# A batched matrix product on one core: paired transposes, a manual order and a rearranged end

## The chip, the cores and the metric

The kernel runs on one core of a Trainium2 chip. The metric is the device time of one execution in microseconds, the median of the runs. Before the change it is 530.44 us (12 runs, 529.81 to 531.82).

## What is computed

The reference multiplies 32 pairs of matrices, all in float32 in memory:

```python
batch, m, k, n = 32, 512, 1024, 768
def reference(x, weight):        # x: 32 x 512 x 1024, weight: 32 x 1024 x 768
    return np.matmul(x, weight).astype(np.float32)
```

A batch reads 2.10 MB of x and 3.15 MB of weights and writes 1.57 MB. Over 32 batches that is 167.77 MB read and 50.33 MB written.

## The kernel before

The batches are worked off in one loop (L51). For each batch, GpSimd issues two transfers that cast to bfloat16 on the way: the weights into `wb_sb` (L53) and x into `x_sb` (L56). Each has three buffers, so loads run up to three batches ahead; a load into a used buffer waits until TensorE has read that buffer for the last time. The weights are laid out with 8 consecutive rows of k on each of the 128 partitions, and x with 4 consecutive rows of m, so a partition reads one contiguous piece of memory per transfer.

A batch consists of four row tiles of 128 rows (the loop over `mt`, L60). TensorE needs x with k on the partitions. So it transposes eight 128x128 blocks of the row tile against an identity matrix (L64), each into its own PSUM tile `pt`, and each is copied to `xT_sb` at once (L69). Then eight matmuls add up 512 output columns in the PSUM tile `pm`, and eight more the other 256 (L74), and each sum is copied to `out_sb` (L81). The copies are given to `nc.any`: the scheduler puts them on VectorE or ScalarE, which decides the order of the instructions on each engine as well. After the four row tiles, SP issues one store of the whole batch (L83). The output tile has three buffers.

[...]

Of the kernel before, what the change touches and what calls it, by code (L numbers as in the profile page):

```python
# [1 line left out]

# [5 lines left out]

F32 = mybir.dt.float32
BF16 = mybir.dt.bfloat16  # L10


@with_exitstack
def kernel(
    ctx: ExitStack,
    tc: tile.TileContext,
    x: bass.AP,
    weight: bass.AP,
    out: bass.AP,
):  # L20
    nc = tc.nc
    B, M, K = x.shape
    _, _, N = weight.shape
    P = 128
    assert M % P == 0 and K % P == 0
    MT = M // P
    KT = K // P

    N_SPLITS = []
    off = 0  # L30
    while off < N:
        sz = min(512, N - off)
        N_SPLITS.append((off, sz))
        off += sz

    const = ctx.enter_context(tc.tile_pool(name="const", bufs=1))
    ident = const.tile([P, P], BF16)
    make_identity(nc, ident)

    w_pool = ctx.enter_context(tc.tile_pool(name="w", bufs=3))  # L40
    x_pool = ctx.enter_context(tc.tile_pool(name="x", bufs=3))
    xT_pool = ctx.enter_context(tc.tile_pool(name="xT", bufs=4))
    out_pool = ctx.enter_context(tc.tile_pool(name="out", bufs=3))
    tpsum = ctx.enter_context(tc.tile_pool(name="tpsum", bufs=4, space=bass.MemoryType.PSUM))
    mpsum = ctx.enter_context(tc.tile_pool(name="mpsum", bufs=4, space=bass.MemoryType.PSUM))

    w_view = weight.rearrange("b (ki ko) n -> b ki ko n", ki=P)
    x_view = x.rearrange("b (mi mo) k -> b mi mo k", mi=P)
    out_view = out.rearrange("b (mi mo) n -> b mi mo n", mi=P)

    for b in range(B):  # L51
        wb_sb = w_pool.tile([P, KT, N], BF16)
        nc.gpsimd.dma_start(out=wb_sb, in_=w_view[b])  # L53

        x_sb = x_pool.tile([P, MT, K], BF16)
        nc.gpsimd.dma_start(out=x_sb, in_=x_view[b])  # L56

        out_sb = out_pool.tile([P, MT, N], F32)

        for mt in range(MT):  # L60
            xT_sb = xT_pool.tile([P, KT, P], BF16)
            for j in range(KT):
                pt = tpsum.tile([P, P], BF16)
                nc.tensor.transpose(  # L64
                    pt,
                    x_sb[:, mt, j::KT],
                    ident,
                )
                nc.any.tensor_copy(xT_sb[:, j, :], pt)  # L69

            for (noff, nsz) in N_SPLITS:
                pm = mpsum.tile([P, nsz], F32)
                for j in range(KT):
                    nc.tensor.matmul(  # L74
                        pm,
                        xT_sb[:, j, :],
                        wb_sb[:, j, noff:noff + nsz],
                        start=(j == 0),
                        stop=(j == KT - 1),
                    )  # L80
                nc.any.tensor_copy(out_sb[:, mt, noff:noff + nsz], pm)  # L81

        nc.sync.dma_start(out_view[b], out_sb)  # L83


# [1 line left out]
_INS = ['x', 'weight']  # L87
_OUTS = [((32, 512, 768), 'float32')]


# [23 lines left out]
```

## Time and profile before

| what | value |
|---|---|
| median of 12 runs | 530.44 us |
| profiled execution, its time | 530.53 us |
| profiled execution, its span | 528.7 us |
| TensorE matmuls busy | 434.7 us, 82% |
| TensorE weight loads busy | 287.8 us, 54% |
| VectorE / ScalarE busy | 103.2 us, 20% / 222.6 us, 42% |
| mean granted TensorE clock | 0.970 |
| bytes written by the DMA engines | 134.72 MB, mean 255 GB/s |
| weights transfer, issue to landing | 34.0 us median |
| store, issue to landing | 14.5 us median |

The span is the time from the first to the last instruction of the profiled execution; its device time is 1.85 us longer. Busy times of matmuls are modelled, so 82% does not say that TensorE runs at 82% of its peak. The GB/s of the page count what lands: a load of float32 that is cast to bfloat16 counts half of what it reads. A DMA share is the mean busy share of the 16 DMA engines; as records of neighbouring packets overlap a little, it can stand slightly above 1.

### The profile page before, as it was taken

To read this page: it belongs to the slowest core of one execution; us is meant where nothing else is said; L and a number is where in the kernel's file an instruction comes from. 1 tells how busy PE (TensorE), PEld (TensorE's weight loads), DVE (VectorE), ACT (ScalarE), POOL (GpSimd) and SP (SyncE) were. 2 spreads that over 40 slices of the span, in tenths; PEclk is the share of its full clock that TensorE was granted. 3 is DMA by queue.
4 is the path that set the end of the run, shared out by engine and by line. 5 is a ranking of instruction groups with operands and counts; after the bars stand their busy time and mean duration, and the time that the engine had idled before them with its cause. 6 is when DMAs were issued, how large, how long until landed. Compare 5 with 4: busy or idle time off the path is not lost.

```text
span 528.7 us, 7878 instructions
## 1 busy us (share of the span) xinstructions
PE 434.7 (82%) x3015; PEld 287.8 (54%) x3072; DVE 103.2 (20%) x515; ACT 222.6 (42%) x766; POOL 34.6 (7%) x70
## 2 busy tenths in 40 slices
PE   0799979877799879789897979788889977988794
PEld 0466656555466556456465656556555654655463
DVE  0122211212122111122121121212121121221111
ACT  0254534444354434345353444434443443444342
POOL 3000000000000000000000000000000000000000
PEclk9999999999899989999898999989998998999899
DMA  8999999999999999999999999999999999999952
GB/s 160 216 222 277 276 262 269 274 274 262 250 254 275 273 270 244 268 257 276 273 249 270 245 274 274 273 261 249 262 267 277 258 269 255 255 273 275 267 189 120
DMA packets 13861, 134.72 MB, mean 255 GB/s; under 512 B 1536, under 2 KB 1536, under 8 KB 1536
## 3 DMA queue, kind: packets, MB, share of 16 engines
q0 software_dynamic: 9216, 83.89, 75.6%
q1 hardware_dynamic: 4608, 50.33, 23.0%
q8 instruction: 24, 0.39, 0.3%
q14 instruction: 13, 0.11, 0.0%
HBM read 167.77 MB, written 50.33 MB: 413 GB/s over the span
## 4 chain that ended last, share of the span: by engine, by line
issue 81%; DMA 9%; POOL 6%; PE 2%; POOLq 0%; DVE 0%; ACT 0%
DMA wb_sb<-in_weight_dram 7%; POOL wb_sb L53 3%; POOL x_sb L56 3%; DMA x_sb<-in_x_dram 3%; PE pm L74 2%; PE pt L64 0%; DVE xT_sb L69 0%; POOLq L53 0%; POOLq L56 0%; ACT out_sb L81 0%; POOL ident masks.py:199 0%; POOL ident masks.py:197 0%; POOLq masks.py:199 0%; POOLq L109 0%; POOLq L98 0%
## 5 line engine op out<-in xcount | busy, mean ns | idle before, releaser
L74 PE MATMUL pm<-wb_sb,xT_sb 128*128 128x512 bf16 (+1 forms) x1991 | 382.2, 334 | 47.5 <-DMA wb_sb<-in_weight_dram 44.4
L74 PEld LDWEIGHTS <-xT_sb 128*128 128x128 bf16 x2048 | 200.4, 100 | 158.1 <-issue 48.9
L81 ACT COPY out_sb<-pm 128x512 f32<-128x512 f32 (+1 forms) x256 | 122.5, 479 | 207.4 <-PE pm L74 192.9
L69 DVE COPY xT_sb<-pt 128x128 bf16<-128x128 bf16 x515 | 103.2, 221 | 417.0 <-PE pt L64 402.7
L64 PE MATMUL pt<-ident,x_sb 128*128 128x128 bf16 x1024 | 126.4, 226 | 40.0 <-DVE xT_sb L69 22.3
L69 ACT COPY xT_sb<-pt 128x128 bf16<-128x128 bf16 x509 | 112.0, 273 | 92.0 <-PE pt L64 91.6
L64 PEld LDWEIGHTS <-x_sb 128*128 128x128 bf16 x1024 | 102.1, 148 | 76.2 <-issue 48.8
L56 POOL DMA_DIRECT2D x_sb<-in_x_dram x32 | 17.0, 530 | 385.5 <-PE pt L64 385.5
L53 POOL DMA_DIRECT2D wb_sb<-in_weight_dram x32 | 17.1, 533 | 54.2 <-PE pt L64 53.8
L69 ACT ACT_TABLE_LOAD x1 | 1.3, 1283 | 0.7 <-PEq L98 0.7
masks.py:199 POOL TENSOR_SCALAR_AFFINE_SELECT ident<-ident 128x128 bf16<-128x128 bf16 x1 | 0.3, 305 | 0.1
masks.py:197 POOL MEMSET ident<- 128x128 bf16 x1 | 0.2, 204 | 0.3 <-POOLq L98 0.3
L98 POOL MEMSET const-float32-0.0<- 128x1 f32 x1 | 0.1, 98 | 0.2 <-issue 0.2
L98 POOL MEMSET const-bfloat16-1.0<- 128x1 bf16 x1 | 0.1, 101 | 0.0
L98 POOL MEMSET const-uint8-127<- 128x1 uint8 x1 | 0.1, 101 | 0.0
L98 POOL MEMSET const-float32-1.0<- 128x1 f32 x1 | 0.1, 98 | 0.0
## 6 DMA issues: line engine op xcount, KB each, us to landing
wb_sb<-in_weight_dram POOLq DMA_DIRECT2D x32, 1536.0 KB, 34.0
out_dram<-out_sb SPq DMA_DIRECT2D x32, 1536.0 KB, 14.5
x_sb<-in_x_dram POOLq DMA_DIRECT2D x32, 1024.0 KB, 27.3
```

The lines of the kernel that those rows point to most:

```text
L53: nc.gpsimd.dma_start(out=wb_sb, in_=w_view[b])
L56: nc.gpsimd.dma_start(out=x_sb, in_=x_view[b])
L64: nc.tensor.transpose(pt, x_sb[:, mt, j::KT], ident,)
L69: nc.any.tensor_copy(xT_sb[:, j, :], pt)
L74: nc.tensor.matmul(pm, xT_sb[:, j, :], wb_sb[:, j, noff:noff + nsz], start=(j == 0), stop=(j == KT - 1),)
L81: nc.any.tensor_copy(out_sb[:, mt, noff:noff + nsz], pm)
L98: nc = _bacc.Bacc("TRN2", target_bir_lowering=False, num_devices=1)
```

## The change

The kernel fixes the order by hand (`manual_schedule`) and changes these things:

- **Transposes.** x in bfloat16 is read as pairs, one 4-byte float32 element for two neighbours in k. Four transposes of 128x128 four-byte elements into one PSUM bank take the place of eight two-byte ones (L64 of the new kernel). One copy on VectorE of 1024 two-byte elements takes the whole row tile out of PSUM (L66). The two members of a pair lie next to each other there, so a matmul reads its weights with a step of two elements.
- **PSUM and eviction.** Two row tiles share three PSUM banks (1536 columns). ScalarE copies out the first 1024 columns, VectorE the last 512, once for each pair of row tiles. The 512-column and 256-column matmuls alternate.
- **Buffers and order of loads.** x, weights and output have five buffers instead of three. x comes before the weights of its batch, and the loads of batch b + 4 are issued at the start of batch b. The identity is made after batch 0's loads are issued.
- **The last four batches.** Their weights are loaded in chunks of rows, two of four rows each, for the last batch four, two and two. All four row tiles work through a chunk before the next chunk begins, into two PSUM tiles at once. The transposes of the next batch stand between the row tiles of the last chunk. The stores of batches 28, 29 and 30 are issued by GpSimd behind the last load. The last batch is stored by SP in two halves, one for each pair of row tiles.

The core of the diff:

```diff
+    CHUNKED = {B - 4: (4, 4), B - 3: (4, 4), B - 2: (4, 4), B - 1: (4, 2, 2)}
+    HELD = {B - 4, B - 3, B - 2}
...
+    def load_w(b):
+        ws[b] = w_pool.tile([P, KT, N], BF16, name="w_sb")
+        at = 0
+        for n in CHUNKED.get(b, (KT,)):
+            nc.gpsimd.dma_start(out=ws[b][:, at:at + n, :], in_=w_view[b, :, at:at + n, :])
+            at += n
...
+    def transpose(b, mt):
+
+        pt = tpsum.tile([P, JT, P], F32, name="pt")
+        pairs = xs[b].bitcast(F32)
+        for j in range(JT):
+            nc.tensor.transpose(pt[:, j, :], pairs[:, mt, j::JT], ident)
+        xT = xT_pool.tile([P, JT, P, 2], BF16, name="xT")
+        nc.vector.tensor_copy(
+            xT.rearrange("p j m r -> p (j m r)"), pt.bitcast(BF16).rearrange("p j m -> p (j m)")
+        )
+        return xT
...
+    def evacuate(b, pair, pm):
+        o = outs[b]
+        nc.scalar.copy(o[:, pair * N2:pair * N2 + 1024], pm[:, 0:1024])
+        nc.vector.tensor_copy(o[:, pair * N2 + 1024:(pair + 1) * N2], pm[:, 1024:N2])
...
+        for b in range(B):
+            if b + 4 < B:
+                load_x(b + 4)
+                load_w(b + 4)
+            outs[b] = out_pool.tile([P, MT * N], F32, name="out_sb")
+            if b not in CHUNKED:
+                xT = {mt: transpose(b, mt) for mt in (0, 1)}
+                for pair in range(2):
+                    pm = mpsum.tile([P, N2], F32, name="pm")
+                    for half in range(2):
+                        if pair == 0:
+                            matmuls(pm, half, xT[half], b, range(KT), False)
+                            xT[2 + half] = transpose(b, 2 + half)
+                        else:
+                            matmuls(pm, half, xT[2 + half], b, range(KT), False)
+                    evacuate(b, pair, pm)
+                nc.sync.dma_start(out_view[b], outs[b])
+                continue
+            xT = ready.pop(b, None) or {mt: transpose(b, mt) for mt in range(MT)}
+            pms = [mpsum.tile([P, N2], F32, name="pm") for _ in range(2)]
+            at = 0
+            for n in CHUNKED[b]:
+                last = at + n == KT
+                for mt in range(MT):
+                    if last and b + 1 < B:
+                        ready.setdefault(b + 1, {})[mt] = transpose(b + 1, mt)
+                    matmuls(pms[mt // 2], mt % 2, xT[mt], b, range(at, at + n), True)
+                    if last and mt % 2 == 1:
+                        pair = mt // 2
+                        evacuate(b, pair, pms[pair])
+                        if b not in HELD:
+                            cols = slice(pair * N2, (pair + 1) * N2)
+                            nc.sync.dma_start(out_view[b, :, cols], outs[b][:, cols])
+                at += n
+            if b in HELD:
+                nc.gpsimd.dma_start(out=out_view[b], in_=outs[b])
```

More of the change, by code (lines that the diff above doesn't have):

```diff
@@ L24 @@
     P = 128
-    assert M % P == 0 and K % P == 0
     MT = M // P
     KT = K // P
[L29 to L34, printed above, removed]
-    const = ctx.enter_context(tc.tile_pool(name="const", bufs=1))
[L37 to L42, printed above, removed]
@@ L43 @@
-    out_pool = ctx.enter_context(tc.tile_pool(name="out", bufs=3))
-    tpsum = ctx.enter_context(tc.tile_pool(name="tpsum", bufs=4, space=bass.MemoryType.PSUM))
-    mpsum = ctx.enter_context(tc.tile_pool(name="mpsum", bufs=4, space=bass.MemoryType.PSUM))
+    JT = KT // 2
+    N2 = 2 * N
+    CHUNKED = {B - 4: (4, 4), B - 3: (4, 4), B - 2: (4, 4), B - 1: (4, 2, 2)}
+    HELD = {B - 4, B - 3, B - 2}
+    const = ctx.enter_context(tc.tile_pool(name="const", bufs=1))
+    w_pool = ctx.enter_context(tc.tile_pool(name="w", bufs=5))
@@ L47 @@
+    x_pool = ctx.enter_context(tc.tile_pool(name="x", bufs=5))
+    xT_pool = ctx.enter_context(tc.tile_pool(name="xT", bufs=8))
+    out_pool = ctx.enter_context(tc.tile_pool(name="out", bufs=5))
+    tpsum = ctx.enter_context(tc.tile_pool(name="tpsum", bufs=2, space=bass.MemoryType.PSUM))
+    mpsum = ctx.enter_context(tc.tile_pool(name="mpsum", bufs=2, space=bass.MemoryType.PSUM))
     w_view = weight.rearrange("b (ki ko) n -> b ki ko n", ki=P)
     x_view = x.rearrange("b (mi mo) k -> b mi mo k", mi=P)
-    out_view = out.rearrange("b (mi mo) n -> b mi mo n", mi=P)
@@ L51 @@
[L51 to L67, printed above, removed]
-                )
[L69 to L83, printed above, removed]
+    out_view = out.rearrange("b (mi mo) n -> b mi (mo n)", mi=P)
@@ new lines, with load_x @@
+    xs, ws, outs = {}, {}, {}
+    def load_x(b):
+        xs[b] = x_pool.tile([P, MT, K], BF16, name="x_sb")
+        nc.gpsimd.dma_start(out=xs[b], in_=x_view[b])
+    def load_w(b):
[14 more added lines that the diff above has]
+        return xT
@@ new lines, with matmuls @@
+    SPLITS = (((0, 512), (512, N - 512)), ((0, 1024 - N), (1024 - N, N2 - 1024)))
+    def matmuls(pm, half, xT, b, kos, together):
+        for ko in kos:
+            for i, (off, size) in enumerate(SPLITS[half]):
+                shares = half == 1 and i == 0
+                nc.tensor.matmul(
+                    pm[:, half * N + off:half * N + off + size],
+                    xT[:, ko // 2, :, ko % 2],
+                    ws[b][:, ko, off:off + size],
+                    start=(ko == 0 and not (together and shares)),
+                    stop=(ko == KT - 1),
+                    skip_group_check=together,
+                )
@@ new lines, in evacuate @@
+    def evacuate(b, pair, pm):
+        o = outs[b]
+        nc.scalar.copy(o[:, pair * N2:pair * N2 + 1024], pm[:, 0:1024])
+        nc.vector.tensor_copy(o[:, pair * N2 + 1024:(pair + 1) * N2], pm[:, 1024:N2])
+    with tc.manual_schedule():
+        load_x(0)
+        load_w(0)
+        ident = const.tile([P, P], F32)
+        make_identity(nc, ident)
+        for b in range(1, 4):
+            load_x(b)
+            load_w(b)
+        ready = {}
+        for b in range(B):
[34 more added lines that the diff above has]
+                nc.gpsimd.dma_start(out=out_view[b], in_=outs[b])
```

## The prediction

> **What bounds the kernel now.** I read the page's slices first: which resource is full, and where it stops being full. Then the queue table, the windows cut at the places where the DMA row changes, the waits, and last TensorE's rows inside one batch. From the page, slices and queue table:
>
> ```profile
> PE   0799979877799879789897979788889977988794
> DMA  8999999999999999999999999999999999999952
> ...
> q0 software_dynamic: 9216, 83.89, 75.6%
> q1 hardware_dynamic: 4608, 50.33, 23.0%
> HBM read 167.77 MB, written 50.33 MB: 413 GB/s over the span
> ```
>
> The DMA row is full from the second slice to the third last and then drops to 5 and 2. TensorE has 7s and 8s throughout. The two queues add up to 98.6% of 16 engines' span, that is 521.3 us of packet time per engine in a span of 528.7. No edit that leaves the bytes alone can take much from the middle. The windows (columns: length, busy time and count of PE, PEld, DVE, ACT, POOL, then clock, DMA share, GB/s) show what is left at the end:
>
> ```profile
> 20.00:500.00 480.00, 411.12 (x2852) 271.97 (x2906) 97.01 (x483) 209.16 (x724) 30.59 (x58) 0.97 1.02 263
> 500.00:504.60 4.60, 4.37 (x36) 3.17 (x36) 0.80 (x4) 2.31 (x7) 0.00 (x0) 1.00 1.03 264
> 504.60:509.10 4.50, 3.77 (x31) 2.51 (x29) 1.38 (x7) 2.44 (x9) 0.00 (x0) 1.00 0.36 76
> 509.10:513.20 4.10, 3.87 (x29) 2.68 (x30) 0.98 (x5) 1.97 (x8) 0.00 (x0) 1.00 0.92 384
> 513.20:519.70 6.50, 6.10 (x47) 4.15 (x47) 1.36 (x8) 3.21 (x12) 0.00 (x0) 1.00 0.01 3
> 519.70:522.70 3.00, 2.59 (x19) 1.42 (x17) 0.29 (x2) 1.39 (x4) 0.00 (x0) 1.00 0.00 0
> 522.70:527.50 4.80, 0.00 (x0) 0.00 (x0) 0.00 (x0) 0.00 (x0) 0.00 (x0) 1.00 0.78 328
> ```
>
> A share of 1.02 is a full DMA system (records of neighbouring packets overlap by 2%). It is full until 504.6. In the 22.9 us from there to 527.5 it works 1.62 + 3.77 + 0.07 + 0 + 3.74 = 9.2 us. So 13.7 us are empty, because TensorE has a whole batch to compute after the last weights land, and two stores come late: the second last batch's between 509 and 513, the last one's after 522.7. The waits, and a piece of TensorE's timeline within one batch, give its own pace:
>
> ```profile
> PE pm L74 <- DMA wb_sb<-in_weight_dram: 44.4, 29, 3.2
> ...
> 486.99 0.38 PE L74 MATMUL pm<-wb_sb,xT_sb 128*128 128x512 bf16 x1
> 487.20 0.35 PE L64 MATMUL pt<-ident,x_sb 128*128 128x128 bf16 x3
> 487.39 2.55 PE L74 MATMUL pm<-wb_sb,xT_sb 128*128 128x512 bf16 x14
> 489.77 0.42 PE L64 MATMUL pt<-ident,x_sb 128*128 128x128 bf16 x4
> ```
>
> TensorE waits for weights in 29 batches, 1.5 us each. A row tile's 16 matmuls take 489.77 - 486.99 = 2.78 us less 0.19 for the three transposes between them, so 2.6, or 10.4 us for a batch of four. A batch's DMA period is 4.19 MB (2.62 loaded as bf16, 1.57 stored) over 263 GB/s = 15.9 us.
>
> **The change, part by part.**
>
> The DMA floor of the new kernel. The bytes stay. The stores of batches 28 to 30 move onto GpSimd's queue behind the last load, and five buffers instead of three let loads be issued four batches ahead. If nothing empties the DMA system after 504.6, the 9.2 us of work (over 1.02: 9.0) follow at once: the mean engine ends at 513.6. The slowest engine ends later: the 0.36 window puts the mean engine's end of the last weights at 504.6 + 1.6 = 506.2, while the matmul that waits for them starts at 509.06, so the slowest lags by some 2.7 us. From the last packet to the end of the span it is now 528.7 - 527.5 = 1.2 us. Floor: 513.6 + 2.7 + 1.2 = 517.5 us. The cuts add packets: five more weight DMAs and one more store. Estimate 0.4 us, from 0.0 (overlapped) to 1.0.
>
> The start. x of batch 0 goes ahead of its weights, and the identity is made behind both. The first transfer is issued at 1.3 us in both kernels, and the DMA system is full from then on, so this is worth 0 for the end (between -0.3 and +0.3); TensorE's earlier start is no gain while loads set the pace.
>
> Transposes: 1024 two-byte ones become 512 four-byte ones, 16 a batch, and here the trace has no row. Nearest below: two-byte transposes, four in 0.41 us, 0.10 each. [...] I take 0.2, twice the row for twice the bytes, and keep 0.1 to 0.41. A batch on TensorE is then 10.4 + 16 x 0.2 + a stall of 0.4 = 14.0 us, against 15.9; with 0.41 it is 17.4. The stall is the first transpose group's copy behind VectorE's last eviction; before, such waits were 22.3 us in all. Cost in the middle: nothing, hidden by the loads, with 1.9 us of cover.
>
> Copies. 1024 copies of 128x128 (221 and 273 ns) become 128 of 128x1024 on VectorE, and ScalarE keeps 64 of 128x1024. ScalarE's two forms, 585 ns for 512 columns and 372 for 256, give 0.83 ns a column, so about 1.0 us each: 2.0 us a batch. VectorE: estimate 1.2 us x 4 + 0.6 x 2 = 6.0 us a batch. Both lie beside 15.9. ScalarE's load falls and gains nothing, since nobody waits for it now. Two row tiles in three banks: a pair's eviction (1.0 us) has the other pair's 5.2 us of matmuls as cover. Weights of the matmuls are now read with a step of two elements; the old transposes already load with a step of eight at 0.09 us each (five in 0.45), so 0, or up to the double where a load would show.
>
> Queues. On SP only stores remain; the last batch's two halves stand behind store 27, which is long done. On GpSimd each held store waits for its batch's eviction, and behind it stands nothing but the next held store. Loads are not held up by these waits.
>
> The tail, counted from the landing of batch 27's weights. The load queue reads 167.77 MB in 75.6% of 528.7 us of packet time, 420 GB/s, so the loads of 28 to 31 take 12.5 us each, plus 6.2 us for what is left of stores 26 and 27 among them: the last chunk lands at about 56.5. TensorE: batch 27's rest 12.0, all four transpose groups of 28 to 15.2, then its first half as that chunk lands and its second half with 29's transposes to 28.8; batches 29 and 30 at 13.6 each give 42.4 and 56.0; batch 31's three chunks end at 66.4. Its eviction is out by 67.4. Meanwhile the DMA system has three stores of 3.75 us behind the last load, to 67.8. So the last stores are there when it comes free: loss about 0. With 0.25 us a transpose TensorE ends 3 us later and the loss is 0.7; with 0.30 it is 4. I take 0.2.
>
> Sum: 517.5 + 0.4 + 0.2 = 518.1 us of span. The profiled execution took 530.53 us for a span of 528.7, so 1.85 lie around it; its time equals the median of the runs (530.44) within 0.1. Predicted: 520.0.
>
> **The rivals.**
>
> First, TensorE lags in the tail only. Between 0.25 and 0.32 us a transpose it still keeps up with mixed loads and stores (15.9 a batch), but not with the bare loads at the end (12.5). It would carry a lag of several us into the last batch, and the DMA system would go empty between held stores: 521.5 to 526, at 0.30 some 524. For it: 1.9 us of cover is not much. Against: half the instructions.
>
> Second, on the other side: TensorE becomes the bound. The mechanism is the four-byte transpose, its place is each batch, its price 16 t. It decides from 10.4 + 0.4 + 16 t = 15.9, so t = 0.32 us. [...] For: the row only covers two bytes.
>
> Third, the change does not keep the DMA system full: if packets get slower by 2% with eight loads in flight, 10 us are lost and it ends at 528 to 531. Against: the share stays 1.02 to 1.03 in windows with quite different mixtures.
>
> **How the numbers follow.** The likeliest, the DMA floor with a hidden tail: 0.71, 520.0, its own range 517 to 522.5 (the lag of the slowest engine may vanish, -2.7; packets and tail +2). The lag in the tail: 0.13. TensorE bound: 0.12, slower. No gain: 0.04, split. The range 516.5 to 526 takes in the first two with their bounds and leaves out some 0.16. A measurement of this kernel tells about 0.2% from no change. Faster 0.84, same 0.03, slower 0.13.
>
> **What would show it.** The DMA row at 9 up to the last slice but one; the weights' waits on TensorE larger than 44 us in total; a four-byte transpose at or under 0.25 us each in TensorE's timeline; the last load landing some 11 us earlier than 509 (by three stores); and no window after it with a share under 0.9 until the slowest engine's end. It is wrong if TensorE never waits for weights, if transposes take over 0.32 us, or if the DMA row has holes in the last three slices.

## The result and the profile after

The changed kernel takes 520.92 us (median of 8 runs, 520.02 to 522.08), against 530.28 for the kernel before beside it (32 runs). The ratio is 0.9815, 95% interval 0.9802 to 0.9828. 520.0 was predicted, within a range of 516.5 to 526. The profiled execution has a span of 518.9 us and a time of 520.73.

From the page of the changed kernel, slices and queue table:

```profile
PE   1788789878888887898788978779887889789894
DMA  8999999999999999999999999999999999999995
...
q0 software_dynamic: 10368, 88.61, 79.3%
q1 hardware_dynamic: 4320, 45.61, 21.2%
...
HBM read 167.77 MB, written 50.33 MB: 420 GB/s over the span
```

The DMA row is now full up to the last slice but one, and the last slice reads 5; before, the last two read 5 and 2. The page counts the packet time of both queues against the same 16 DMA engines. The three held stores have moved from one queue to the other. The two shares now add up to 100.5% of the span, or 521.5 us of packet time, where it was 521.3: the same work in a shorter span. The windows of the changed kernel, with the same columns as before (PE, PEld, DVE, ACT, POOL, then clock, DMA share, GB/s):

```profile
20.00:500.00 480.00, 407.61 (x2421) 266.96 (x2467) 119.40 (x185) 61.75 (x61) 32.20 (x61) 0.94 1.02 261
500.00:508.00 8.00, 7.95 (x52) 5.01 (x53) 2.00 (x4) 1.01 (x1) 0.53 (x1) 1.00 0.99 417
508.00:510.00 2.00, 2.00 (x14) 1.17 (x12) 0.00 (x0) 0.00 (x0) 0.00 (x0) 1.00 0.68 289
510.00:512.00 2.00, 2.00 (x15) 1.18 (x12) 0.00 (x0) 0.99 (x1) 0.00 (x0) 1.00 0.20 86
512.00:514.00 2.00, 0.28 (x2) 0.00 (x0) 1.33 (x2) 1.04 (x2) 0.00 (x0) 1.00 0.24 98
514.00:517.60 3.60, 0.00 (x0) 0.00 (x0) 0.05 (x1) 0.00 (x0) 0.00 (x0) 0.65 0.94 382
```

The middle has not moved: its share is 1.02 as before, at 261 GB/s where it was 263. The 13.7 empty microseconds at the end have become about 4: (1 - 0.68) x 2 + (1 - 0.20) x 2 + (1 - 0.24) x 2 = 3.8 us between 508 and 514. While they pass, TensorE is at the last batch's matmuls, and the last batch's two stores cannot start. So the gap was not closed entirely. Why it is there shows in the chain of work that ended last (start, duration, what):

```profile
435.05 47.10 DMA x_sb<-in_x_dram
482.14 0.05 issue
482.19 0.75 PE pt L64 x4
...
506.91 5.38 PE pm L78 x32
512.29 0.02 issue
512.31 1.02 ACT out_sb L89
513.33 0.02 issue
513.36 0.69 DVE out_sb L90
```

From 482.2 to 512.3 the chain lies on TensorE without a break (its other pieces are TensorE's too); then come the last two evictions. This stretch begins with a transpose that waited for x of batch 30. TensorE's own timeline shows that wait:

```profile
473.25 6.66 PE L78 MATMUL pm<-w_sb,xT 128*128 128x256 bf16 x40
482.19 0.75 PE L64 MATMUL pt<-ident,x_sb 128*128 128x128 f32 x4 [2.28 <-DMA x_sb<-in_x_dram]
482.78 1.46 PE L78 MATMUL pm<-w_sb,xT 128*128 128x512 bf16 x7
484.08 0.65 PE L64 MATMUL pt<-ident,x_sb 128*128 128x128 f32 x4
484.56 1.46 PE L78 MATMUL pm<-w_sb,xT 128*128 128x256 bf16 x8
```

TensorE stands idle for 2.28 us, from 479.9 to 482.2, ahead of a transpose of batch 30. The matmuls queued behind it belong to batch 29. Their second chunk was issued at 428.2, ahead of that x (435.1), on the same queue. Where the transpose doesn't stand in front of them (e3 below), these matmuls start without a wait at about 480. So they were ready.

### The profile page after: what moved, and what is told of

Read it like the earlier page. It is cut to its first block, busy times and chain, and to the rows that moved or that the text cites. A ratio compares the mean times of both kernels' runs of the same rounds, so it can differ in the third digit from the quotient of the medians.

```text
span 518.9 us, 5796 instructions
## 1 busy us (share of the span) xinstructions
PE 425.0 (82%) x2512; PEld 277.5 (53%) x2560; DVE 124.2 (24%) x192; ACT 66.1 (13%) x65; POOL 38.9 (7%) x78
## 4 chain that ended last, share of the span: by engine, by line
PE 63%; another core or an unknown queue 18%; DMA 12%; issue 3%; ACT 1%; DVE 1%; POOL 1%; DVEq 0%; POOLq 0%
PE pm L78 55%; DMA x_sb<-in_x_dram 9%; PE pt L64 8%; DMA w_sb<-in_weight_dram 3%; ACT out_sb L89 1%; DVE xT L66 1%; POOL w_sb L56 1%; POOL x_sb L50 0%; DVE out_sb L90 0%; DVEq L66 0%; POOLq L50 0%; POOLq L56 0%; POOLq L152 0%
## 5 line engine op out<-in xcount | busy, mean ns | idle before, releaser
L78 PE MATMUL pm<-w_sb,xT 128*128 128x256 bf16 (+1 forms) x2000 | 372.6, 341 | 73.9 <-DMA w_sb<-in_weight_dram 58.3
L78 PEld LDWEIGHTS <-xT 128*128 128x128 bf16 x2048 | 207.9, 102 | 213.7 <-issue 58.2
L66 DVE COPY xT<-pt 128x1024 bf16<-128x1024 bf16 x128 | 85.1, 686 | 232.2 <-PE pt L64 232.2
L89 ACT COPY out_sb<-pm 128x1024 f32<-128x1024 f32 x64 | 64.8, 1012 | 446.5 <-PE pm L78 446.5
L64 PE MATMUL pt<-ident,x_sb 128*128 128x128 f32 x512 | 79.1, 288 | 13.4 <-DMA x_sb<-in_x_dram 11.9
L64 PEld LDWEIGHTS pt<-ident,x_sb 128*128 128x128 f32 x512 | 75.6, 207 | 20.7 <-issue 11.2
L90 DVE COPY out_sb<-pm 128x512 f32<-128x512 f32 x64 | 43.9, 686 | 157.7 <-ACT out_sb L89 157.7
L56 POOL DMA_DIRECT2D w_sb<-in_weight_dram x37 | 19.7, 531 | 242.3 <-DMA w_sb<-in_weight_dram 206.4
L137 POOL DMA_DIRECT2D out_dram<-out_sb x3 | 1.6, 533 | 29.5 <-DVE out_sb L90 29.5
```

Source lines behind the costliest of these rows:

```text
L56: nc.gpsimd.dma_start(out=ws[b][:, at:at + n, :], in_=w_view[b, :, at:at + n, :])
L64: nc.tensor.transpose(pt[:, j, :], pairs[:, mt, j::JT], ident)
L66: nc.vector.tensor_copy(xT.rearrange("p j m r -> p (j m r)"), pt.bitcast(BF16).rearrange("p j m -> p (j m)"))
L78: nc.tensor.matmul(pm[:, half * N + off:half * N + off + size], xT[:, ko // 2, :, ko % 2], ws[b][:, ko, off:off + size], start=(ko == 0 an ...
L89: nc.scalar.copy(o[:, pair * N2:pair * N2 + 1024], pm[:, 0:1024])
L90: nc.vector.tensor_copy(o[:, pair * N2 + 1024:(pair + 1) * N2], pm[:, 1024:N2])
```

## The experiments

Three theories of the gain were open: that it all lies in the end; that the order, the transposes or the buffers win time in the middle; and, within the end, whether the chunks or the held stores do it. For the rest of the gap there were two: the order of TensorE's instructions, or the slowest DMA engine.

**e1, the end as in a plain batch.** Manual order, pairs, five buffers and merged evictions stay.

```diff
-    CHUNKED = {B - 4: (4, 4), B - 3: (4, 4), B - 2: (4, 4), B - 1: (4, 2, 2)}
-    HELD = {B - 4, B - 3, B - 2}
+    CHUNKED = {}
+    HELD = set()
```

> The manual order, paired transposes, five buffers and merged evictions are kept; the end is as in a plain batch (no row chunks, no held stores, the last batch stored whole). The theory that the gain is all in the end (DMA full in the middle of both kernels) expects little: the last weights land on the slowest engine at about 509 us, then a whole batch on TensorE (10.3 and two transpose groups 1.0), eviction 1.7, a whole store 3.8 and its end 1.5, so a span of 527 and a time of 528 to 529, 1 to 2 us under before. The rival, that the order or the transposes win time in the middle, expects 524 or less.

Measured: 531.32 us, ratio to before 1.0010 (0.9995 to 1.0025). No gain at all, so the theory of the end holds, and the rival of the middle falls: five buffers, half the transposes and 64 large evictions in place of hundreds of small copies are together worth nothing measurable. A slower end does not hide a gain of the middle either: by the packets in the trace the last load lands at 508.0, before at 508.7, so the middle gave at most 0.7 us. The time came out 2 to 3 us above my expectation. The last batch is not a plain 10.4 us of matmuls:

```profile
505.25 1.11 PE L64 MATMUL pt<-ident,x_sb 128*128 128x128 f32 x8
508.48 4.44 PE L78 MATMUL pm<-w_sb,xT 128*128 128x512 bf16 x15 [2.12 <-DVE xT L66]
512.76 0.65 PE L64 MATMUL pt<-ident,x_sb 128*128 128x128 f32 x4
513.24 2.76 PE L78 MATMUL pm<-w_sb,xT 128*128 128x256 bf16 x16
```

After the transposes the matmuls wait 2.12 us for VectorE's copies, and the first row tile of matmuls takes 4.44 us where the next takes 2.76. The windows show a granted TensorE clock of 0.90 from 505 to 510, 0.76 from 510 to 515 and 1.00 from 515 to 520.

**e2, chunks without held stores**, and **e5**, the same with the transposes moved as in e3 below.

```diff
-    HELD = {B - 4, B - 3, B - 2}
+    HELD = set()
```

With no held stores the code sends batches 28 to 30 out in two halves each, as it does the last batch.

> Chunks kept; the stores of batches 28 to 30 are issued by SP in their turn instead of by GpSimd behind the last load. The theory that the held stores are what fills the DMA engines while TensorE finishes expects a loss: loads end some 8 to 10 us later (last chunk on the slowest engine at about 510), then 2.6 us of matmuls, 1.7 of eviction, half a store 1.9 and its end 1.5, so a span of 518 to 520 and a time of 520 to 522: the same or up to 1 us slower than the changed kernel, because chunks alone already leave little after the last landing. The rival, that holding the stores is the main part of the gain, expects 525 or more.

> Stores of batches 28 to 30 in their turn on SP, as in e2, and the late transposes of e3 as well. In e2 TensorE waited 3.3 and 1.7 us for x of the next batch with ready matmuls behind. If that head-of-line wait was what the held stores had bought off, the loss of e2 (5.6 us) mostly goes: 520 to 522. If the held stores are worth it because they give the DMA engines work while TensorE finishes the last batch, TensorE still ends about 10 us after its last weights and nothing is left to move by then: 523.5 to 525.5.

Measured: e2 526.48 us (ratio 0.9926, 0.9899 to 0.9954), e5 525.44 (0.9906, 0.9890 to 0.9922). My expectation for e2 was wrong, and its rival was right: the chunks alone leave more than half of the gain undone. In e5 the waits for x shrink, the longest from 3.32 us to 2.04, and little comes of it: the two intervals overlap. The chain of e5 no longer runs over these waits, but from the landing of the last batch's first chunk. The end of e5, TensorE's timeline and two windows:

```profile
505.61 10.57 PE L78 MATMUL pm<-w_sb,xT 128*128 128x512 bf16 x63 [0.87 <-DMA w_sb<-in_weight_dram]
```

```profile
505.00:510.00 5.00, 4.39 (x28) 2.70 (x29) 1.18 (x2) 0.00 (x0) 0.00 (x0) 1.00 0.93 274
510.00:515.00 5.00, 4.95 (x32) 2.96 (x31) 0.00 (x0) 0.08 (x1) 0.00 (x0) 1.00 0.14 56
```

I had counted 2.6 us of matmuls after the last chunk. But TensorE can start the last batch only with its first chunk, at 505.61, and needs 10.6 us from there, while the other two chunks take only half a batch of weights' transfer time. Once they have landed, the DMA engines have next to nothing to do (share 0.14). Cutting the weights does not remove TensorE's last batch; other traffic has to be moved under it. Whether it matters that GpSimd issues the held stores, and not SP at the same moments, was not tested.

**e3, the next batch's transposes behind ready matmuls.**

```diff
                 for mt in range(MT):
-                    if last and b + 1 < B:
-                        ready.setdefault(b + 1, {})[mt] = transpose(b + 1, mt)
                     matmuls(pms[mt // 2], mt % 2, xT[mt], b, range(at, at + n), True)
+                    if last and b + 1 < B and mt >= 2:
+                        for t in (2 * mt - 4, 2 * mt - 3):
+                            ready.setdefault(b + 1, {})[t] = transpose(b + 1, t)
```

> In the last four batches the next batch's transposes stand behind the third and the fourth row tile instead of ahead of each, so that TensorE does not wait for x of batch 30 (2.28 us at 482.2) with matmuls queued behind that are ready. The theory that TensorE's in-order queue sets the end of the changed kernel (chain of work: TensorE without a break from 482.2 to 512.3) expects its end 2 to 2.5 us earlier and the span 1.5 to 2.2 us shorter: 518.7 to 519.5. The rival, that the DMA floor on its slowest engine sets the end, expects no change: 520.5 to 521.3.

Measured: 518.83 us (518.64 to 518.86), ratio to before 0.9774 (0.9757 to 0.9791), which does not overlap the interval of the changed kernel. TensorE ends at 509.6 instead of 512.3 and the span is 517.0. The place of the transposes in TensorE's order was indeed the cause of these 2 us.

**e12, TensorE earlier still.** On top of e3, the transposes of batch 28 stand behind the last two row tiles of batch 27.

```diff
+                            if b + 1 == B - 4:
+                                for t in (2 * half, 2 * half + 1):
+                                    ready.setdefault(b + 1, {})[t] = transpose(b + 1, t)
```

> As e3, with the four transpose groups of batch 28 behind the last two row tiles of batch 27 instead of all together at the start of 28, where TensorE waits 1.5 us for VectorE's copies. TensorE should end about 2 us earlier, at 507.5. If the slowest DMA engine sets the end of e3 (it leaves the held stores at 512 and has 3.8 us of stores to go), nothing changes: 518.5 to 519.1. If TensorE still sets the end, 516.7 to 517.5.

Measured: 518.81 us (0.9784, 0.9770 to 0.9797). TensorE's last piece in e3, then in e12:

```profile
499.05 10.56 PE L78 MATMUL pm<-w_sb,xT 128*128 128x512 bf16 x63
...
497.49 10.56 PE L78 MATMUL pm<-w_sb,xT 128*128 128x512 bf16 x64
```

TensorE ends at 508.1, 1.5 us earlier than in e3, and the time does not move. In e3 TensorE no longer sets the end.

**e4 and e11, the DMA traffic alone.** There are no transposes, matmuls or evictions; the stores write zeros, and each of them waits only for its batch's loads (the last ones not even for these).

```diff
+            o = out_pool.tile([P, MT * N], F32, name="out_sb")
+            nc.vector.memset(o, 0.0)
+            if b < B - 1:
+                nc.vector.tensor_copy(o[:, 0:1], ws[b][:, KT - 1, 0:1])
+                nc.vector.tensor_copy(o[:, 1:2], xs[b][:, MT - 1, 0:1])
...
```

e11 sets `HELD = set()` as well and lets the store of batch 30 go without waiting.

> No transposes, matmuls or evictions; every load and store of the changed kernel stays, in the same queues, each store waiting for its batch's loads (its bytes are zeros), the last batch's stores not waiting for its loads. It measures the DMA floor. The prediction's floor with the slowest engine's lag of 2.7 us expects a span of 517.5 to 518 and a time of 519.4 to 519.9; if that lag is not additive (the gap before the last stores swallowed it in the changed kernel), 515 to 516 and 517 to 518.

> As e4 (only loads and stores, no work on TensorE), but no store goes through GpSimd and the last transfer to end is one of SP's. In e4 the last landing came 3.7 us before the end of the span, where it is 0.9 us in kernels that end on SP. If that is the price of ending on GpSimd's queue, the DMA floor itself is about 514.2 of span and 516 of time. If not, it stays at 517 and 518.6.

Measured: 518.59 us for e4 (ratio 0.9771, 0.9754 to 0.9788) and 518.92 for e11 (0.9782, 0.9760 to 0.9803), both with spans of 516.9. The span lies between the two expectations, 0.6 us from the prediction's floor, but for another reason. The last windows of e4 (here DVE, POOL, clock, DMA share, GB/s):

```profile
508.00:510.00 2.00, 0.00 (x0) 0.00 (x0) 1.00 1.04 442
510.00:512.00 2.00, 0.00 (x0) 0.00 (x0) 1.00 0.95 406
512.00:514.00 2.00, 0.00 (x0) 0.00 (x0) 1.00 0.05 18
514.00:516.90 2.90, 0.00 (x0) 0.00 (x0) 1.00 0.00 0
```

and of e3 (PE, PEld, DVE, ACT, POOL, clock, DMA share, GB/s):

```profile
508.00:510.00 2.00, 1.61 (x10) 0.72 (x8) 0.61 (x1) 1.37 (x2) 0.00 (x0) 1.00 0.58 246
510.00:512.00 2.00, 0.00 (x0) 0.00 (x0) 0.77 (x2) 0.66 (x1) 0.00 (x0) 1.00 0.70 292
512.00:514.00 2.00, 0.00 (x0) 0.00 (x0) 0.00 (x0) 0.00 (x0) 0.00 (x0) 1.00 1.00 409
514.00:517.00 3.00, 0.00 (x0) 0.00 (x0) 0.00 (x0) 0.00 (x0) 0.00 (x0) 0.61 0.27 111
```

With traffic alone all 16 engines are full to about 512 (share 0.95 from 510 to 512, then 0.05) and done together: by the packets in the trace, the engines end within 0.9 us of one another, and the last landing comes at 513.2. The remaining 3.7 us of e4's span are no DMA. SP's waits put 3.0 us of them (3.1 in e11) down to TensorE's sequencer at the end of the program. In the changed kernel that wait is 0.7; why it differs is open. e11 ends the same way, and it did not tell whether GpSimd's queue has a part in it, because its last landing was again one of GpSimd's, a load. In e3 the 16 engines end the last held store between 508.1 and 511.9, a spread of 3.8 us. The slowest still has 3.75 us of stores to do, and its last packet indeed ends at 515.6. The landing is signalled at 516.0, and 1.0 us later the span ends, at 517.0. So the floor of the pure traffic is about 513.2 + 1.0 = 514.2 of span (an estimate: e4's last landing, and the 1.0 us that e3 takes from its last landing to the end). The working kernel does not reach it because some engines lag, and, by e12, not because of TensorE.

What makes them lag is not shown. Beside a few smaller packets, the queue tables of e3 and e4 differ in one line, which e3 has and e4 lacks:

```profile
q8 instruction: 20, 0.33, 0.2%
```

The table of the changed kernel has the same line. Its 20 packets take 0.93 us each, 18.5 us in all, and start between 32.7 and 501.7 us. The 16 landings of a load lie 1.1 us apart there at 49 us, 2.9 at 145 and 4.5 at 335. Whether these packets have a part in that, no run separates.

**e6, held stores without chunks**, on top of e3.

```diff
-    CHUNKED = {B - 4: (4, 4), B - 3: (4, 4), B - 2: (4, 4), B - 1: (4, 2, 2)}
+    CHUNKED = {B - 4: (KT,), B - 3: (KT,), B - 2: (KT,), B - 1: (KT,)}
```

> As e3 (held stores, late transposes), but the weights of the last four batches come in one transfer each, so no matmul of a batch starts before all its rows are there. If chunks matter because they let TensorE start each of the last batches early, it loses about 3 us at batch 29 and one more later (weights of 29 land at about 477.5, its matmuls could start at 474.4), ends at about 513 instead of 509.6, and the time is 521 to 522.5. If TensorE lags behind the loads anyway, chunks are worth nothing once the stores are held: 518.5 to 519.3.

Measured: 519.60 us (0.9802, 0.9782 to 0.9821), 0.8 us over e3, with overlapping intervals. This lies between the two theories, and nearer to the second: once the stores are held, the chunks are worth about 1 us. TensorE waits 2.39 us for the weights of batch 29 (about 3 were expected), but after that its lag swallows the rest. It starts the last batch at 501.15 without a wait, 0.7 us behind the weights' last packet, and ends at 511.7, not at 513.

**e7 and e8, the cost of the transposes.** In the changed kernel every group of transposes is done twice, in e8 three times (`range(3)`).

```diff
-        for j in range(JT):
-            nc.tensor.transpose(pt[:, j, :], pairs[:, mt, j::JT], ident)
+        for _ in range(2):
+            for j in range(JT):
+                nc.tensor.transpose(pt[:, j, :], pairs[:, mt, j::JT], ident)
```

> The changed kernel with every transpose done twice (the second writes the same values again): 16 more four-byte transposes a batch at the measured 0.12 us, 0.24 us in place of 0.12. TensorE's batch becomes 10.4 + 3.9 + 0.4 = 14.7, under the loads' 15.9, so the middle should hide it; in the last four batches it lies on the path, about 1.9 us for each of three and the same ahead of batch 28, less the wait for x that it covers (2.3): span 5 to 6 us longer, 525 to 527. If the middle has no cover, 32 x 1.9 = 61 us more.

> The changed kernel with every transpose done three times: 0.36 us in place of 0.12, beyond the point (0.32) from which the prediction's second rival says that TensorE is the bound. TensorE's batch is then 10.4 + 5.8 + 0.4 = 16.6 us: 15 + 32 x 16.6 + 4.6 = 551 of span, time 553, and TensorE no longer waits for weights. If the prediction's stall or matmul time was mis-sized, the time tells by how much per batch (1 us a batch is 32 us).

Measured: e7 524.90 us (0.9895, 0.9880 to 0.9910), 4.0 over the changed kernel: the doubled transposes cost nothing in the middle (DMA share 1.02, 261 GB/s as in the changed kernel) and about 4 us in the end, less than the 5 to 6 expected. e8 541.75 us in one run, 21 more than the changed kernel, where 553 was expected. TensorE's timeline of e8 over one batch:

```profile
306.58 3.05 PE L65 MATMUL pt<-ident,x_sb 128*128 128x128 f32 x24
309.47 2.76 PE L79 MATMUL pm<-w_sb,xT 128*128 128x512 bf16 x16
312.07 1.61 PE L65 MATMUL pt<-ident,x_sb 128*128 128x128 f32 x12
313.52 2.76 PE L79 MATMUL pm<-w_sb,xT 128*128 128x256 bf16 x15
...
322.76 3.05 PE L65 MATMUL pt<-ident,x_sb 128*128 128x128 f32 x24
```

Twelve transposes occupy 313.52 - 312.07 = 1.45 us, 0.12 each. The batch takes 322.76 - 306.58 = 16.2 us, more than the loads' 15.9, and TensorE has no gap left: it waits 2.1 us for weights in the whole run, where the changed kernel waits 58.3. That is 10.4 + 5.8 without the stall of 0.4 (the waits of e8 list none of TensorE for VectorE); with 16.2 in place of 16.6 the sum of 15 + 32 P + 4.6 is 538 of span, and 539.9 was measured. The 15 us for the first batch to land and the 4.6 for eviction, store and end are my estimates, the 15 from the load queue's 420 GB/s; in the changed kernel the first matmul starts at 16.8. The prediction's second rival is real. Its point was put at 0.32 us, and the runs enclose it between 0.24 (no cost in the middle) and 0.36.

**e9, two-byte transposes**, and **e10, three buffers**, each on top of e3. Core of e9:

```diff
+        pt = tpsum.tile([P, KT, P], BF16, name="pt")
+        for j in range(KT):
+            nc.tensor.transpose(pt[:, j, :], xs[b][:, mt, j::KT], ident)
```

e10 sets `bufs=3` for x and weights and loads two batches ahead instead of four.

> As e3, with the two-byte transposes back: eight 128x128 bfloat16 ones for a row tile instead of four four-byte ones, one copy of 1024 elements as before. The theory that the middle is bound by loads and the end by the slowest DMA engine expects no change as long as eight two-byte transposes take no more than 1 us: 518.3 to 520. If the paired transposes are a part of the gain, 522 or more.

> As e3, with three buffers of x and weights instead of five and loads issued two batches ahead instead of four. If the DMA queue was never empty with three buffers (share 1.02 in the middle before the change), nothing changes: 518.3 to 519.5. If deep prefetch keeps the DMA engines busier, 521 or more.

Measured: e9 518.78 us (0.9779, 0.9761 to 0.9797), the same as e3. TensorE's timeline of e9:

```profile
471.69 1.13 PE L63 MATMUL pt<-ident,x_sb 128*128 128x128 bf16 x16
472.65 1.46 PE L77 MATMUL pm<-w_sb,xT 128*128 128x256 bf16 x8
```

Sixteen two-byte transposes occupy 472.65 - 471.69 = 0.96 us, as eight four-byte ones do in e3: 0.06 us each against 0.12, so pairing gains nothing on TensorE.

e10 520.44 (0.9814, 0.9792 to 0.9836), 1.6 over e3, between the two expectations. Its middle is the same (share 1.02, 262 GB/s). The loss comes in through GpSimd's queue, whose timeline in e10 reads:

```profile
459.12 1.05 POOL L56 DMA_DIRECT2D w_sb<-in_weight_dram  x2 [4.67 <-PE pm L78]
476.65 0.54 POOL L138 DMA_DIRECT2D out_dram<-out_sb  x1 [16.48 <-DVE out_sb L90]
477.17 0.53 POOL L50 DMA_DIRECT2D x_sb<-in_x_dram  x1
477.70 1.59 POOL L56 DMA_DIRECT2D w_sb<-in_weight_dram  x3
```

With loads only two batches ahead, the held store of batch 28 stands in front of the last batch's loads and holds them back until its eviction; x of the last batch then lands late (TensorE waits 1.10 us for it), and TensorE ends at 511.6. So what the deeper look-ahead is worth here comes from the end: it puts the last loads ahead of the held stores.

## Why the prediction was right, point by point

- **The middle is bound by the DMA engines and stays so.** Right: the share is 1.02 in every run, e1 brings no gain, and e7, e9 and e10 change nothing there. TensorE waits for weights 58.3 us in all instead of 44.4, as foretold. The third rival, slower packets with more loads in flight, did not come: 521.5 us of packet time after 521.3.
- **The floor of 517.5 plus 0.4.** Right in mechanism, about 1 us too high: e3 and e12 reach spans of 517.0 and 516.8. The slowest engine was put 2.7 us behind the mean one, because a matmul's start (509.06) was read as its end. By the 16 landings of the last load it is 2.2 us behind the mean before and 2.1 in the changed kernel. The cuts' 0.4 us stood on no row, and the runs give no sign of it.
- **Transposes 0.2 us each.** Mis-sized: 0.12. The row was misread: "four in 0.41 us" is how long the group lasts, and not the spacing. Three of them occupy 487.39 - 487.20 = 0.19 us in the prediction's own lines, 0.06 each, and it takes just this 0.19 off for the matmuls. Twice the row for twice the bytes would have given 0.12, and a factor of 2 is what was measured: 0.06 for two bytes (e9), 0.12 for four (e3, e7, e8). The upper end of 0.41, and the 17.4 us a batch with it, are shown by no run; the doubled and tripled transposes of e7 and e8 still take 0.12 each (eight in 0.96 us, twelve in 1.45). What sets the 0.12, no run separates.
- **A stall of 0.4 us a batch behind VectorE.** Mis-sized: 1.5 us, as the piece of the changed kernel's timeline below shows. The 1.2 us for a copy of 1024 columns on VectorE was an estimate without a row; the copy takes 686 ns in bfloat16. But the eviction of 512 columns on VectorE, 686 ns as well, takes place after ScalarE's 1.0 us, not beside it (the chain above: ACT from 512.31 to 513.33, then DVE from 513.36), and the transposes' copies queue behind it. The cover of the middle (TensorE's 10.4 + 1.9 + 1.5 = 13.8 against 15.9) hides it. In the end it counts twice: at batch 28's start, and at the last eviction, which takes 1.7 us and not 1.0.
- **The tail's loss of 0.2.** This step failed: the gap is 3.8 us long, and e3 shows that 2.1 us of it could be won. The step said that TensorE runs batches 29 and 30 at 13.6 us without waiting, and ends at 66.4 after the landing of batch 27's weights (444.3), so at 510.7. It ended at 512.3. It left out the wait of 2.28 us for x with ready matmuls behind it, the full stall ahead of batch 28, and the clock: batch 27 itself took 14.2 us where 12.0 was put, its first 15 matmuls 5.3 us at a granted clock of 0.50 (444.2 to 449.4). The cheaper transposes gave most of that back. In kind this is the first rival, a lag of TensorE in the tail, but not by slow transposes. That rival's prices don't follow from the working either: at 0.25 us a transpose TensorE's eviction would end 3 us later, at 70.4, against the stores' 67.8, a loss of 2.6 us and not 0.7.
- **What would show it.** Three signs came as said: the DMA row, the weights' waits, and a transpose under 0.25 us. The last load landed at 500.8, which is where the tail's working has it (56.5 after 444.3), but 8 us earlier than before, not 11. The last sign failed: windows with shares of 0.68, 0.20 and 0.24 stand behind it.
- The two errors, a floor 1 us too high and a tail 2 us too good, have opposite signs. The predicted 520.0 lies within 1 us of the measured time partly by that luck.

The shorter TensorE batch leaves longer waits for weights (58.3 us in 21, where it was 44.4 in 29), as the changed kernel's timeline shows:

```profile
301.10 5.28 PE L78 MATMUL pm<-w_sb,xT 128*128 128x512 bf16 x16 [3.81 <-DMA w_sb<-in_weight_dram]
306.17 0.93 PE L64 MATMUL pt<-ident,x_sb 128*128 128x128 f32 x4
306.94 2.76 PE L78 MATMUL pm<-w_sb,xT 128*128 128x256 bf16 x15
...
317.80 2.45 PE L78 MATMUL pm<-w_sb,xT 128*128 128x512 bf16 x13 [1.48 <-DVE xT L66]
```

After a wait of 3.81 us the first 16 matmuls take 5.28 us, about twice the 2.76 of the next row tile. The granted clock is 0.50 from 301.0 to 306.3 and 1.00 from 306.9 to 309.7. Its mean over the span fell from 0.970 to 0.937, while the DMA share of the middle stayed at 1.02.

## What to carry to other kernels

When the DMA engines are full, ask what they do while the compute engine finishes its last batch, and move stores that can wait behind the last load. Here that was worth 5.6 us (e2 against the changed kernel) to 6.6 (e5 against e3), and no other edit was worth as much once it was in place. Row chunks let the last batch start early, but its whole compute time still follows its first chunk; with the stores held they were worth 0.8 us (e3 against e6). Where an engine works in order, put the preparation of the next batch behind work that is already fed (2.1 us in e3), and put look-ahead loads ahead of stores that wait on the same queue (1.6 us in e10).

## What the runs showed of the hardware that I had not expected

- A copy of 1024 bfloat16 columns out of PSUM on VectorE takes 686 ns, the same as one of 512 float32 columns.
- TensorE's mean granted clock was 0.970 before, 0.937 in the changed kernel and 0.991 with doubled transposes (e7), with 44.4, 58.3 and 30.6 us of waits for weights. The wait of 3.81 us at 301.1 was followed by matmuls at half pace (clock 0.50); so was one of 1.99 us in e7 (15 matmuls in 4.44 us), but not the one of 2.28 us at 482.2 (clock 1.00 from 478 to 484.5). The length of the wait alone does not decide it. Ahead of e7's wait stood 16 transposes, so that 3.9 us passed without a matmul; at 482.2 it was 2.9. But 3.6 us of that kind, around 460, did not slow the matmuls behind them either (clock 1.00 from 456 to 463). What decides it, these runs do not show.
- The 16 DMA engines end their last load 4.3 us apart before, their last held store 3.1 us apart in the changed kernel and 3.8 in e3, and they end within 0.9 us of one another in e4, which only moves data.
